# A PEER decoder layer: 192 instead of 128 tokens by gathered expert rows, 320 in the dense part with v as stationary operand

## Chip, cores and metric

The kernel runs on one core of one Trainium2 chip. The metric is the device time of one execution in microseconds (us), the median of the runs shown; lower is better.

## What is computed

One decoder layer on 512 tokens of width 1024, in fp32: normed input projection, three groups of attention heads, output projection and residual, and then the PEER feed-forward, which is all that the change touches. Each token picks 16 of 16384 experts for each of 8 heads; an expert is one row of `u` and one of `v`.

```python
def peer_ffn(h, w_q, sub1, sub2, u, v):
    qry = (h @ w_q).reshape(B, S, PEER_HEADS, PEER_DKEY)
    ...
    v1, i1 = lax.top_k(s1, PEER_TOPK)
    v2, i2 = lax.top_k(s2, PEER_TOPK)
    ...
    top_s, pos = lax.top_k(cand, PEER_TOPK)
    expert = jnp.take_along_axis(cand_idx, pos, axis=-1)
    gate = jax.nn.softmax(top_s, axis=-1)
    ...
        a = jnp.einsum('cd,ced->ce', x_c, u[e_c])
        w = jax.nn.gelu(a.astype(jnp.float32), approximate=False).astype(x_c.dtype) * g_c
        return jnp.einsum('ce,ced->cd', w, v[e_c])
```

## The kernel before

The 512 tokens are four chunks of 128. Projection, attention and output projection come first (to about 300 us) and are untouched. After them the kernel treats the feed-forward in two ways.

**Chunk 0 by gathered rows.** `route` (L411) finds 128 experts and gates for every token. `gather_all` (L477) is a Python generator of 256 steps. A u step has GpSimd (POOL) issue an indirect DMA that brings, for slot s, one row of u for each of the 128 tokens into a tile `row` (512 KB, four buffers, L473); VectorE (DVE) multiplies it with the normed tokens `hg` and sums (L480). After 128 of them a Gelu and a product give the weights `gw`, and 128 v steps add weighted rows of v into `ga[0]` (L487).

**Chunks 1 to 3 densely.** All 16384 experts are computed for 384 tokens, in 128 blocks b of 128 experts. A *first product* (`a_block`, L515) multiplies a block of u with the tokens: 24 matmuls of 384 moving columns into a bank `t`, then a Gelu on ScalarE (ACT). All products have three matmuls per operand pair (`mm3`, L91), because an fp32 operand is split into a high and a low part: ScalarE copies the high part, VectorE subtracts (`split`, L83; `u_parts`, L508). The first products of blocks 0 to 63 are computed early and parked in HBM (`ad`). The gates come from one-hots: VectorE makes two one-hot rows per token (L584, L585), TensorE (PE) multiplies them (L588), and the resulting table goes to HBM (`gd`, L590). A *second product* (`w_block`, L616) loads a block of v and its slice of the gate table (`gt`), multiplies Gelu and gate into `w` (L632), splits v and w, and adds `w` times v into six PSUM banks that hold 384 x 1024 outputs: 18 matmuls of 512 columns, with w as stationary operand (L635 to L638). I call the stretch of second products the dense part.

The order on each engine comes from a scheduler that simulates the program; every engine then runs its instructions in that fixed order, and SP issues nearly all plain DMAs in order. The early first products each release one gather step (L596); the rest of the generator is emptied at the end of the program text (L654), and the scheduler mixes those steps with the dense part.

Of the kernel before, what the change touches and what calls it, by code (L numbers as in the profile page):

```python
# [22 lines left out]
P = 128  # L23
S = 512
# [22 lines left out]
GR = 1.0  # L47
TD = P * len(DC)
GROUPS = ((0, 1, 2), (3, 4, 5), (6, 7))
# [5 lines left out]
def layer_kernel(ctx, tc, x, xT, memT, mem, w_in, w_kv, w_out, w_q, cols, qk_gain, g_bc, subT, bias_tab,  # L55
# [9 lines left out]
    st = ctx.enter_context(tile_pool(name="st", bufs=8))  # L65
    xd = [dram.tile([P, D], F32, name=f"xd{c}") for c in range(NT)]
    gd = dram.tile([TD // GT, P, NK, GT], F32, name="gd")
# [51 lines left out]
    def quarters(t):  # L119
        return t.rearrange("p (a b) -> p a b", b=P)  # L120
# [232 lines left out]
    def mix_out(chunks, yT, rg, hT, name):  # L353
        n_c = len(chunks)
        with tile_pool(name=f"wo{name}", bufs=2) as wo:
# [26 lines left out]
            for i, c in enumerate(chunks):  # L382
                if i == 1:
                    for k2 in range(KD // 2):
                        w_piece(0, k2)
                DMA.dma_start(xd[c], xs[i])
# [83 lines left out]

    def gather(table, s_):
        row = gr.tile([P, D], F32, tag="row", name="row")
        G.indirect_dma_start(out=row, out_offset=None, in_=table,  # L473
                             in_offset=bass.IndirectOffsetOnAxis(ap=exp_g[:, s_:s_ + 1], axis=0))
        return row

    def gather_all():  # L477
        for s_ in range(NSLOT):
            row = gather(u, s_)
            V.scalar_tensor_tensor(row, row, 1.0, hg, ALU.mult, ALU.mult, accum_out=av[:, s_:s_ + 1])  # L480
            yield
        ge = peer.tile([P, NSLOT], F32, name="ge")
        A.activation(ge, av, AF.Gelu)
        V.tensor_mul(gw, ge, gate_g)
        for s_ in range(NSLOT):
            row = gather(v, s_)
            V.scalar_tensor_tensor(ga[0], row, gw[:, s_:s_ + 1], ga[0], ALU.mult, ALU.add)  # L487
            yield

# [24 lines left out]

    def a_block(b):  # L515
        us = halves.pop(b)
        ap = bank("t")[:, :TD]
        for k in range(KD):
            mm3(ap, [t[:, k, :] for t in us], [t[:, k, S - TD:] for t in hT], k == 0, k == KD - 1)
        ag = ub.tile([P, TD], F32, tag="ag", name="ag", bufs=3)  # L520
        A.activation(ag, ap, AF.Gelu)  # L521
        return ag

    with tile_pool(name="qa", bufs=1) as qa, tile_pool(name="qp", bufs=2) as qp:
        mix_out([GC] + DC, yT, rg, hT, "l")
        G.memset(ga[0], 0.0)
        rp = ctx.enter_context(tile_pool(name="rp", bufs=1, side="right"))
        sub = qa.tile([P, 2 * PH, NK], F32, name="sub", bufs=1)
        for n in range(4):
# [25 lines left out]
            for i in range(4):  # L555
                m = 4 * n + i
                acc = bank("s")[:, :TD]
                for k in range(KD):
                    mm3(acc, [t[:, i, k % 2, :] for t in w[k // 2]], [t[:, k, S - TD:] for t in hT],
                        k == 0, k == KD - 1)  # L560
                qy = qp.tile([P, TD], F32, tag="qy", name="qy")
                A.activation(qy, acc, AF.Copy)
                sc = quarters(bank("o"))[:, 0:len(DC), :]
                for j in range(len(DC)):
                    T.matmul(sc[:, j, :], qy[:, j * P:(j + 1) * P], sub[:, m, :], start=True, stop=True)
                sx = qa.tile([P, 4, P], F32, tag="sx", name="sx", bufs=SCB)[:, 0:len(DC), :]
# [34 lines left out]
    with tile_pool(name="vb", bufs=2) as vb:  # L601
        acc = [[bank("ssssoo"[2 * c + n]) for n in range(2)] for c in range(len(DC))]
        inl, spl = (list(range(r0, r1, NB)) for r0, r1 in ((NSP, NK), (0, NSP)))
# [12 lines left out]
        def w_block(n, b, ag):  # L616
# [17 lines left out]
            split(ws[0], ws[1], w)  # L634
            for ci_ in range(len(DC)):  # L635
                for k in range(2):
                    mm3(acc[ci_][k], [t[:, ci_ * P:(ci_ + 1) * P] for t in ws],
                        [t[:, k * 512:(k + 1) * 512] for t in vs], n == 0, n == NK - 1)  # L638

        pend = None  # L640
        for n, b in enumerate(order):
            if b >= NSP:
                for a in (b, later.get(b)):
                    if a is not None and a not in halves and a >= loaded:
                        u_parts(a, a % 2, V)
                        loaded = a + 1
                ag = a_block(b)
# [8 lines left out]
        for c in [GC] + DC:  # L656
            xr = vb.tile([P, D], F32, tag="xr", name="xr", bufs=3)
            DMA.dma_start(xr, xd[c])
            if c == GC:
                V.tensor_add(xr, xr, ga[0])  # L660
            else:
                for k in range(2):
                    sl = xr[:, k * 512:(k + 1) * 512]
                    V.tensor_add(sl, sl, acc[DC.index(c)][k])
            DMA.dma_start(out[c * P:(c + 1) * P, :], xr)

# [58 lines left out]
```

## Time and profile before

| | us |
|---|---|
| median of 3 runs (1699.19 to 1702.47) | 1700.5 |
| the profiled execution | 1706.93 |
| its span, first to last instruction | 1705.2 |
| busy TensorE / VectorE / ScalarE / GpSimd | 1615.1 / 1322.7 / 675.1 / 500.4 |
| DMA, 390.04 MB | mean 229 GB/s |

The span is that of the profiled execution. Busy time of TensorE is modelled, and successive matmuls overlap, so durations of single matmuls are not their cost; the distance between two starts is. `PEclk` is the clock that TensorE was granted, as a share of 2.4 GHz. "out<-in" names the tiles an instruction writes and reads; a matmul's are output, moving and stationary operand.

### The profile page before, as it was taken

What the parts mean: (1) busy time and instruction counts of PE and PEld (TensorE: products, weight loads), DVE (VectorE), ACT (ScalarE), POOL (GpSimd) and SP (SyncE); (2) the same over time, 40 slices, a digit from 0 to 9 for tenths busy, and PEclk for the clock granted to TensorE, in tenths of its full rate; (3) what the DMA queues carried; (4) which work ended last, traced back from release to release, by engine and by line L of the source; (5) the groups of instructions that cost most, each with busy time, mean ns of one, the idle gap of its engine ahead of it and who ended that gap; (6) DMA issues with size and microseconds to landing.
All of it is one profiled execution on the core that took longest, in us unless ns stands there. A gap on an engine that the chain in (4) does not pass through costs nothing.

```text
span 1705.2 us, 23275 instructions
## 1 busy us (share of the span) xinstructions
PE 1615.1 (95%) x8045; PEld 1402.8 (82%) x8045; DVE 1322.7 (78%) x3271; ACT 675.1 (40%) x1031; POOL 500.4 (29%) x338
## 2 busy tenths in 40 slices
PE   7999989998999898988786999999999999999998
PEld 6886667998999897887565888888888888888887
DVE  6656746699999999989996788788887878844444
ACT  7345534233434435444452333333333333333332
POOL 4320013252325232654103343334443333200000
PEclk9999989999999999998897999999999999999999
DMA  8302034133888675675439999999998999854542
GB/s 320 117 27 106 1 115 157 50 112 104 273 282 283 229 279 199 222 278 197 197 141 386 328 349 326 318 345 332 346 333 326 329 349 336 302 195 150 184 146 79
DMA packets 164373, 390.04 MB, mean 229 GB/s; under 512 B 12704, under 2 KB 87456, under 8 KB 161568
## 3 DMA queue, kind: packets, MB, share of 16 engines
q1 hardware_dynamic: 127392, 254.33, 42.9%
q0 software_dynamic: 36864, 134.23, 22.0%
q8 instruction: 63, 1.03, 0.2%
q14 instruction: 54, 0.44, 0.1%
HBM read 346.57 MB, written 41.94 MB: 228 GB/s over the span
## 4 chain that ended last, share of the span: by engine, by line
PE 68%; DVE 25%; DMA 4%; ACT 2%; issue 2%; POOL 0%; SPq 0%; DVEq 0%; ACTq 0%
PE s L93 9%; PE s L95 9%; PE s L94 9%; PE t L93 7%; PE t L95 7%; PE t L94 7%; PE o L94 4%; PE o L93 4%; PE o L95 4%; DVE row L480 4%; DVE o L585 4%; DVE yT L85 3%; PE s L588 3%; DVE o L584 3%; PE o L328 2%
## 5 line engine op out<-in xcount | busy, mean ns | idle before, releaser
L93 PE MATMUL t<-hT,yT 128*128 128x384 f32 x1024 | 350.0, 342 | 25.1 <-ACT ag L521 25.0
L95 PE MATMUL t<-hT,yT 128*128 128x384 f32 x1024 | 349.3, 342 | 11.8 <-DVE yT L85 11.8
L94 PE MATMUL t<-hT,yT 128*128 128x384 f32 x1024 | 348.5, 340 | 0.0
L473 POOL DMA_INDIRECT row<-u,exp_g x128 | 189.8, 1483 | 409.4 <-DVE row L480 292.1
L84 ACT ACTIVATE yT<-flat 128x1024 fp32r<-128x1024 f32 x128 | 135.7, 1060 | 264.3 <-PE t L94 130.6
L473 POOL DMA_INDIRECT row<-v,exp_g x128 | 165.3, 1292 | 255.4 <-DVE ga L487 235.7
L93 PEld LDWEIGHTS t<-hT,yT 128*128 128x128 f32 x1024 | 194.7, 190 | 31.6 <-ACT ag L521 27.1
L85 DVE TENSOR_TENSOR yT<-vr,yT 128x1024 fp32r<-128x1024 f32 x128 | 156.4, 1222 | 69.0 <-ACT yT L84 65.7
L95 PEld LDWEIGHTS t<-hT,yT 128*128 128x128 f32 x1024 | 194.6, 190 | 17.4 <-DVE yT L85 14.1
L85 DVE TENSOR_TENSOR yT<-flat,yT 128x1024 fp32r<-128x1024 f32 x128 | 164.7, 1288 | 52.4 <-ACT yT L84 44.6
L94 PE MATMUL s<-yT,ws 128*128 128x512 f32 x512 | 202.7, 396 | 0.0
L94 PEld LDWEIGHTS t<-hT,yT 128*128 128x128 f32 x1024 | 194.7, 190 | 4.5
L84 ACT ACTIVATE ws<-w 128x384 fp32r<-128x384 f32 x128 | 67.1, 525 | 330.2 <-issue 127.3
L95 PE MATMUL s<-yT,ws 128*128 128x512 f32 x512 | 195.2, 396 | 0.0
L480 DVE SCALAR_TENSOR_TENSOR row<-row,hg 128x1024 f32<-128x1024 f32 x128 | 163.7, 1288 | 13.9 <-DMA row<-u,exp_g 13.7
L84 ACT ACTIVATE yT<-vr 128x1024 fp32r<-128x1024 f32 x128 | 134.5, 1051 | 95.9 <-PE o L95 68.2
L93 PE MATMUL s<-yT,ws 128*128 128x512 f32 x512 | 167.8, 396 | 0.0
L588 PE MATMUL s<-o,o 128*128 128x128 f32 x768 | 154.7, 315 | 11.3 <-DVE o L585 8.4
L487 DVE SCALAR_TENSOR_TENSOR ga<-row,gw,ga 128x1024 f32<-128x1024 f32 x128 | 163.6, 1278 | 1.7 <-DMA row<-v,exp_g 1.0
L588 PEld LDWEIGHTS s<-o,o 128*128 128x128 f32 x768 | 122.1, 199 | 42.6 <-issue 18.8
L85 DVE TENSOR_TENSOR ws<-w,ws 128x384 fp32r<-128x384 f32 x128 | 70.5, 556 | 95.1 <-ACT ws L84 90.9
L585 DVE TENSOR_SCALAR o<-iota,iT 128x128 f32<-128x128 f32 x384 | 131.7, 343 | 0.0
(264 smaller groups left out, 2861.0 us busy)
## 6 DMA issues: line engine op xcount, KB each, us to landing
flat<-uT SPq DMA_DIRECT2D x128, 512.0 KB
vr<-v SPq DMA_DIRECT2D x128, 512.0 KB
gd<-stage SPq DMA_DIRECT2D x12, 2048.0 KB
gt<-gd SPq DMA_DIRECT2D x32, 768.0 KB
ad<-ag SPq DMA_DIRECT2D x64, 192.0 KB
agr<-ad SPq DMA_DIRECT2D x64, 192.0 KB
wraw<-w_in SPq DMA_DIRECT2D x8, 1024.0 KB
flat<-w_q SPq DMA_DIRECT2D x16, 512.0 KB
```

The lines of the kernel that those rows point to most:

```text
L84: A.activation(hi, src, AF.Copy)
L85: return (e_lo or V).tensor_sub(lo, src, hi.bitcast(F32))
L93: T.matmul(o, ah, bh, start=start, stop=False)
L94: T.matmul(o, ah, bl, start=False, stop=False)
L95: T.matmul(o, al, bh, start=False, stop=stop)
L328: T.matmul(o_ps[:, q0:W], l, r, start=n_ == 0, stop=n_ == len(mms) - 1)
L473: G.indirect_dma_start(out=row, out_offset=None, in_=table, in_offset=bass.IndirectOffsetOnAxis(ap=exp_g[:, s_:s_ + 1], axis=0))
L480: V.scalar_tensor_tensor(row, row, 1.0, hg, ALU.mult, ALU.mult, accum_out=av[:, s_:s_ + 1])
L487: V.scalar_tensor_tensor(ga[0], row, gw[:, s_:s_ + 1], ga[0], ALU.mult, ALU.add)
L584: V.tensor_scalar(o1[:, j, :], iota, i1, None, ALU.is_equal)
L585: V.tensor_scalar(o2[:, j, :], iota, i2, gate, ALU.is_equal, ALU.mult)
L588: T.matmul(gp[:, j, :], o1[:, j, :], o2[:, j, :], start=True, stop=True)
```

## The change

64 tokens more go by gathered rows: the first half (`HX`) of chunk 1. Their 128 slots are folded so that all 128 partitions work: partitions 0 to 63 hold slots 0 to 63 of a token, partitions 64 to 127 its slots 64 to 127. So `gather_all` has 64 more u steps and 64 more v steps, which accumulate in `ga[1]`, and its order is u of chunk 0, u of the half, v of chunk 0, v of the half. The normed half tokens go through HBM (`hd`) into both halves of `hx`; the experts and gates get there by one ScalarE copy and one DMA each in `route`. At the end the two halves of `ga[1]` are brought together by a DMA into `other`.

The dense part has `TD` = 320 tokens. First products have 320 moving columns and use one fixed bank, `only`. Second products turn the operands around: v is stationary, `w` with 320 columns moves, and the result is transposed, 8 chunks of 128 output columns by 320 tokens. Seven chunks have a bank each; the eighth is in two pieces, 192 and 128 columns, in what is left of two of these banks. At the end the result is copied to `yo`, transposed in 128x128 squares and added to x. All residual loads stand behind the last gather in the program's end.

```diff
-TD = P * len(DC)
+HX = P // 2
+DX = DC[0]
+T0 = (DX * P) + HX
+TQ = P * len(DC)
+TD = S - T0
...
+                if c == DX:
+                    DMA.dma_start(hd, h[0:HX, :])
...
+        if c == DX:
+            for to, src in zip(extra, (ei, gt)):
+                A.activation(to[0:HX, :], src[0:HX, 0:HX], AF.Copy)
+                DMA.dma_start(to[HX:P, :], src[0:HX, HX:P])
...
+    def gather_all(hx, avx, gwx, exp_x, gate_x):
+        sets = ((NSLOT, exp_g, hg, av, gate_g, gw, ga[0]), (HX, exp_x, hx, avx, gate_x, gwx, ga[1]))
...
+        for n, ex, h, a_, gate, g_, to in sets:
+            for s_ in range(n):
+                row = gather(u, ex, s_)
+                V.scalar_tensor_tensor(row, row, 1.0, h, ALU.mult, ALU.mult, accum_out=a_[:, s_:s_ + 1])
+                yield
+            ge = peer.tile([P, n], F32, name=f"ge{n}")
+            A.activation(ge, a_, AF.Gelu)
+            V.tensor_mul(g_, ge, gate)
+        for n, ex, h, a_, gate, g_, to in sets:
+            for s_ in range(n):
+                row = gather(v, ex, s_)
+                V.scalar_tensor_tensor(to, row, g_[:, s_:s_ + 1], to, ALU.mult, ALU.add)
+                yield
...
-    def a_block(b):
+    def a_block(b, to=None):
         us = halves.pop(b)
-        ap = bank("t")[:, :TD]
+        ap = (bank("t") if to is None else to)[:, :TD]
...
+        for i in range(2):
+            DMA.dma_start(hx[i * HX:(i + 1) * HX, :], hd)
...
-            for q in range(P // GT):
+            for q in range(HX // GT if c == DX else 0, P // GT):
...
-        acc = [[bank("ssssoo"[2 * c + n]) for n in range(2)] for c in range(len(DC))]
+        acc = [bank(tag) for tag in "ssssoot"]
+        only = bank("t")
+        parts = [[(acc[j][:, 0:TD], 0, TD)] for j in range(KD - 1)]
+        parts.append([(acc[0][:, TD:S], 0, S - TD), (acc[1][:, TD:2 * TD - (S - TD)], S - TD, TD)])
...
-            for ci_ in range(len(DC)):
-                for k in range(2):
-                    mm3(acc[ci_][k], [t[:, ci_ * P:(ci_ + 1) * P] for t in ws],
-                        [t[:, k * 512:(k + 1) * 512] for t in vs], n == 0, n == NK - 1)
+            for j in range(KD):
+                for o, t0, t1 in parts[j]:
+                    mm3(o, [t[:, j * P:(j + 1) * P] for t in vs], [t[:, t0:t1] for t in ws],
+                        n == 0 and j < KD - 1, n == NK - 1 and j > 1)
...
+        for j in range(KD):
+            V.memset(yo[j][:, TD:], 0.0)
+            for o, t0, t1 in parts[j]:
+                if j % 2:
+                    A.activation(yo[j][:, t0:t1], o, AF.Copy)
+                else:
+                    V.tensor_copy(yo[j][:, t0:t1], o)
+
+        def emit(r0, rows, terms):
             xr = vb.tile([P, D], F32, tag="xr", name="xr", bufs=3)
...
+        other = vb.tile([P, D], F32, tag="xr", name="other", bufs=3)
+        DMA.dma_start(other[0:HX], ga[1][HX:P, :])
+        emit(GC * P, P, [(every, ga[0])])
+        emit(DX * P, HX, [(every, ga[1]), (every, other)])
...
+                for j in range(4):
+                    T.transpose(ps[:, j * P:(j + 1) * P], yo[4 * k + j][:, i:i + P], ident)
```

The scheduler gives the program a new order. On VectorE, before the change, the last gather multiply of all (L487, into `ga`) stands in the middle of the dense part, ahead of the addition of the residual (L660); the `w` of 32 further second products is still to come.

```order
L632 TENSOR_TENSOR w<-agr,gt 128x384
L487 SCALAR_TENSOR_TENSOR ga_1416<-row,gw,ga_1416 128x1024
L85 TENSOR_TENSOR ws_12954<-w,ws_12953 128x384
L85 TENSOR_TENSOR yT_1442<-vr,yT_1441 128x1024
L660 TENSOR_TENSOR xr<-xr,ga_1416 128x1024
L85 TENSOR_TENSOR yT_1442<-flat,yT_1441 128x1024
L632 TENSOR_TENSOR w<-ag,gt 128x384
```

After the change, the end of VectorE's order reads so (`ws` is the last second product's split, L502 a gather multiply, L687 a copy of a finished bank, L693 the additions at the end):

```order
L90 TENSOR_TENSOR yT_1440<-vr,yT_1439 128x1024
L90 TENSOR_TENSOR ws_15252<-w,ws_15251 128x320
L502 SCALAR_TENSOR_TENSOR ga_1414<-row,gw,ga_1414 128x1024 x2
L687 COPY yo_16250<-s 128x320
L687 COPY yo_16252<-o 128x320
L502 SCALAR_TENSOR_TENSOR ga_1414<-row,gw,ga_1414 128x1024
L687 COPY yo_16254<-t 128x320
L687 COPY yo_16248<-s 128x320
L502 SCALAR_TENSOR_TENSOR ga_1414<-row,gw,ga_1414 128x1024 x27
L502 SCALAR_TENSOR_TENSOR ga_1415<-row,gwx,ga_1415 128x1024 x64
L693 TENSOR_TENSOR xr<-xr,ga_1414 128x1024
L693 TENSOR_TENSOR xr<-xr,ga_1415 64x1024
```

94 gather multiplies stand behind the last split of the dense part, where none stood.

On SP the program ended, before, with the loads of the last blocks and three stores of finished tokens:

```order
L627 DMA vr<-v 128x1024 x7
L619 DMA agr<-ad_131 128x384
L627 DMA vr<-v 128x1024
L665 DMA out<-xr 128x1024 x3
```

and now ends so, where `other` reads the finished `ga[1]`:

```order
L651 DMA vr<-v 128x1024
L698 DMA other<-ga_1415 64x1024
L691 DMA xr<-xd 128x1024
L691 DMA xr<-xd 64x1024
L694 DMA out<-xr 128x1024
L694 DMA out<-xr 64x1024
L691 DMA xr<-xd 128x1024 x2
L691 DMA xr<-xd 64x1024
L694 DMA out<-xr 128x1024 x2
L694 DMA out<-xr 64x1024
```

The loads of x moved from the middle of the dense part to behind the last gather. On TensorE the last second product, formerly rows of 512 columns such as `L95 MATMUL o<-yT_1441,ws_14420 128x512`, ends with the eighth chunk's short pieces:

```order
L99 MATMUL t<-ws_15252,yT_1439 128x320
L100 MATMUL t<-ws_15251,yT_1440 128x320
L98 MATMUL s<-ws_15251,yT_1439 128x192
L99 MATMUL s<-ws_15252,yT_1439 128x192
L100 MATMUL s<-ws_15251,yT_1440 128x192
L98 MATMUL s<-ws_15251,yT_1439 128x128
L99 MATMUL s<-ws_15252,yT_1439 128x128
L100 MATMUL s<-ws_15251,yT_1440 128x128
```

The moving operand is `ws` where it was `yT`, and one second product has 27 matmuls where it had 18.

## Rows read from the trace of the kernel before

**Rows 1.** Stretches: us; busy us (xcount) PE, PEld, DVE, ACT, POOL; PEclk; DMA share; GB/s.
```profile
390.00:730.00 340.00, 318.47 (x1847) 307.25 (x1846) 335.98 (x1112) 143.55 (x183) 120.92 (x67) 0.98 0.69 233
730.00:892.00 162.00, 140.00 (x706) 114.34 (x704) 154.80 (x526) 74.65 (x78) 44.88 (x24) 0.92 0.54 204
892.00:910.00 18.00, 0.00 (x0) 0.00 (x0) 9.74 (x18) 1.37 (x2) 11.14 (x8) 0.57 0.89 327
910.00:1057.00 147.00, 146.36 (x686) 127.45 (x687) 114.14 (x169) 53.35 (x74) 50.66 (x43) 0.98 0.96 345
1057.00:1480.00 423.00, 423.00 (x2007) 366.91 (x2006) 342.50 (x372) 148.12 (x202) 165.50 (x129) 1.00 0.94 334
1480.00:1700.00 220.00, 219.57 (x1031) 188.84 (x1029) 103.82 (x128) 74.27 (x100) 0.00 (x0) 1.00 0.48 155
```

**Rows 2.** Line 487: ns min/median/max, first and last start us, shapes.
```profile
L487 DVE SCALAR_TENSOR_TENSOR ga<-row,gw,ga x128: 1272/1277/1287, 1073.9 to 1486.6; 128x1024 f32<-128x1024 f32 x128
```

**Rows 3.** Timeline, TensorE, two products' first rows; columns start us, us, engine, line.
```profile
1560.47 0.33 PE L93 MATMUL t<-hT,yT 128*128 128x384 f32 x1
...
1564.66 0.39 PE L93 MATMUL s<-yT,ws 128*128 128x512 f32 x1
...
1568.87 0.33 PE L93 MATMUL t<-hT,yT 128*128 128x384 f32 x1
```

**Rows 4.** Timeline, VectorE, one-hot stage, 36 pairs between these.
```profile
797.79 0.27 DVE L584 TENSOR_SCALAR o<-iota,iT 128x128 f32<-128x128 f32 x1
...
814.11 0.27 DVE L584 TENSOR_SCALAR o<-iota,iT 128x128 f32<-128x128 f32 x1
```

**Rows 5.** Timeline, VectorE, gather multiplies before the dense part, splits inside.
```profile
902.66 1.23 DVE L480 SCALAR_TENSOR_TENSOR row<-row,hg 128x1024 f32<-128x1024 f32 x1 [6.67 <-DMA row<-u,exp_g]
903.81 0.08 DVE L480 DVE_READ_ACCUMULATOR row<-row,hg 128x1 f32 x1
...
907.95 1.22 DVE L480 SCALAR_TENSOR_TENSOR row<-row,hg 128x1024 f32<-128x1024 f32 x1 [1.41 <-DMA row<-u,exp_g]
...
1057.21 1.21 DVE L85 TENSOR_TENSOR yT<-vr,yT 128x1024 fp32r<-128x1024 f32 x1
1058.35 0.54 DVE L632 TENSOR_TENSOR w<-agr,gt 128x384 f32<-128x384 f32 x1
```

**Rows 6.** Timeline, SP and ACT at the start, the first load.
```profile
1.64 0.42 SPq L150 DMA_DIRECT2D xtr<-xT  x1
...
4.51 1.28 ACT L88 ACT_TABLE_LOAD   x1 [4.51 <-DMA xtr<-xT]
```

**Rows 7.** TensorE's first and last matmul of the dense part; stores.
```profile
910.64 0.69 PE L93 MATMUL t<-hT,yT 128*128 128x384 f32 x1 [18.69 <-ACT ag L521]
...
1699.17 0.40 PE L95 MATMUL o<-yT,ws 128*128 128x512 f32 x1
...
L665 SPq DMA_DIRECT2D out<-xr x4: 332/340/344, 1491.9 to 1701.0; - x4
```

**Rows 8.** Timeline, TensorE, attention, five fp32 transposes.
```profile
142.90 0.71 PE L315 MATMUL t<-ident,p 128*128 128x128 f32 x5
143.45 0.81 PE L296 MATMUL s<-kT,qT 128*128 128x384 f32 x2
```

**Rows 9.** Groups: xcount, busy us, mean ns, idle us before and releaser.
```profile
L473 POOL DMA_INDIRECT row<-v,exp_g x128 | 165.3, 1292 | 255.4 <-DVE ga L487 235.7 <-issue 8.2 <-DVE row L480 8.0
...
L521 ACT ACTIVATE ag<-t 128x384 f32<-128x384 f32 x128 | 61.0, 478 | 31.0 <-PE t L95 16.9 <-issue 11.8 <-ACT stage L589 0.8
```

**Rows 10.** The page's queue of GpSimd: packets, MB, share.
```profile
q0 software_dynamic: 36864, 134.23, 22.0%
```

**Rows 11.** Timeline, GpSimd, gathers of u before the dense part.
```profile
897.10 0.94 POOL L473 DMA_INDIRECT row<-u,exp_g  x1 [0.30 <-issue]
...
899.58 0.94 POOL L473 DMA_INDIRECT row<-u,exp_g  x1 [0.31 <-issue]
904.16 1.81 POOL L473 DMA_INDIRECT row<-u,exp_g  x1 [3.64 <-DVE row L480]
```

More of the change, by code (lines that the diff above doesn't have):

```diff
@@ L65, in layer_kernel @@
     st = ctx.enter_context(tile_pool(name="st", bufs=8))
-    xd = [dram.tile([P, D], F32, name=f"xd{c}") for c in range(NT)]
+    hd = dram.tile([HX, D], F32, name="hd")
+    xd = dram.tile([S, D], F32, name="xd")
     gd = dram.tile([TD // GT, P, NK, GT], F32, name="gd")
@@ L385, in mix_out @@
                         w_piece(0, k2)
-                DMA.dma_start(xd[c], xs[i])
+                DMA.dma_start(xd[c * P:(c + 1) * P, :], xs[i])
                 r = row_rstd(xs[i], f"rh{c}")
@@ L409, in top16, with route @@
             V.max_index(idx[q][:, 8:16], vals[q][:, 8:16], rest[q])
-    def route(c, dst=None, q0=0, nq=PH):
+    def route(c, dst=None, q0=0, nq=PH, extra=()):
         qs = slice(q0, q0 + nq)
@@ L469, in route, with gather @@
         A.activation(dst, tp, AF.Copy)
[L471 to L488, printed above, removed]
+    def gather_all(hx, avx, gwx, exp_x, gate_x):
+        sets = ((NSLOT, exp_g, hg, av, gate_g, gw, ga[0]), (HX, exp_x, hx, avx, gate_x, gwx, ga[1]))
+        def gather(table, ex, s_):
+            row = gr.tile([P, D], F32, tag="row", name="row")
+            G.indirect_dma_start(out=row, out_offset=None, in_=table,
+                                 in_offset=bass.IndirectOffsetOnAxis(ap=ex[:, s_:s_ + 1], axis=0))
+            return row
+        for n, ex, h, a_, gate, g_, to in sets:
[11 more added lines that the diff above has]
+                yield
     lp = ctx.enter_context(tile_pool(name="lp", bufs=1, side="right"))
@@ L525, in layer_kernel @@
         mix_out([GC] + DC, yT, rg, hT, "l")
-        G.memset(ga[0], 0.0)
+        for t in ga:
+            G.memset(t, 0.0)
         rp = ctx.enter_context(tile_pool(name="rp", bufs=1, side="right"))
+        hx = rp.tile([P, D], F32, name="hx")
+        avx, gate_x, gwx = (rp.tile([P, HX], F32, name=n_) for n_ in ("avx", "gate_x", "gwx"))
+        exp_x = rp.tile([P, HX], I32, name="exp_x")
+        for i in range(2):
+            DMA.dma_start(hx[i * HX:(i + 1) * HX, :], hd)
         sub = qa.tile([P, 2 * PH, NK], F32, name="sub", bufs=1)
@@ L556, in layer_kernel @@
                 m = 4 * n + i
-                acc = bank("s")[:, :TD]
+                acc = bank("s")[:, :TQ]
                 for k in range(KD):
-                    mm3(acc, [t[:, i, k % 2, :] for t in w[k // 2]], [t[:, k, S - TD:] for t in hT],
+                    mm3(acc, [t[:, i, k % 2, :] for t in w[k // 2]], [t[:, k, S - TQ:] for t in hT],
                         k == 0, k == KD - 1)
-                qy = qp.tile([P, TD], F32, tag="qy", name="qy")
+                qy = qp.tile([P, TQ], F32, tag="qy", name="qy")
                 A.activation(qy, acc, AF.Copy)
@@ L589, in layer_kernel @@
                     A.activation(stage[:, :, t4:t4 + 4].rearrange("p e t -> p t e"), gp, AF.Copy)
-                DMA.dma_start(gd[ci_ * (P // GT) + q], stage)
+                DMA.dma_start(gd[(c * P - T0) // GT + q], stage)
         for b in range(NSP):
@@ L646, in layer_kernel @@
                         loaded = a + 1
-                ag = a_block(b)
+                ag = a_block(b, only)
             else:
@@ L655, in layer_kernel @@
             pass
-        for c in [GC] + DC:
-            xr = vb.tile([P, D], F32, tag="xr", name="xr", bufs=3)
[L658 to L665, printed above, removed]
+        yo = [vb.tile([P, TQ], F32, tag=f"yo{j}", name=f"yo{j}", bufs=1) for j in range(KD)]
+        for j in range(KD):
[6 more added lines that the diff above has]
+        def emit(r0, rows, terms):
+            xr = vb.tile([P, D], F32, tag="xr", name="xr", bufs=3)
+            DMA.dma_start(xr[0:rows], xd[r0:r0 + rows, :])
+            for sl, t in terms:
+                V.tensor_add(xr[0:rows, sl], xr[0:rows, sl], t[0:rows])
+            DMA.dma_start(out[r0:r0 + rows, :], xr[0:rows])
+        every = slice(0, D)
+        other = vb.tile([P, D], F32, tag="xr", name="other", bufs=3)
+        DMA.dma_start(other[0:HX], ga[1][HX:P, :])
+        emit(GC * P, P, [(every, ga[0])])
+        emit(DX * P, HX, [(every, ga[1]), (every, other)])
+        for i in range(0, TD, P):
+            terms = []
+            for k in range(2):
+                ps = bank("so"[k])
+                for j in range(4):
+                    T.transpose(ps[:, j * P:(j + 1) * P], yo[4 * k + j][:, i:i + P], ident)
+                terms.append((slice(k * 512, (k + 1) * 512), ps))
+            emit(T0 + i, min(P, TD - i), terms)
 def _bias_table():
```

6 lines of the change are left out of this document (3 added, 3 removed).

## Prediction, made blind

> **What bounds the kernel now.** I read the page's queue table for sizes, the table of stretches first, then the matrix engine's timeline in the dense part, then the gather rows of GpSimd and VectorE, then the last microseconds. In the table of stretches [rows 1] VectorE is full from 390 to 892 us (336 of 340, 155 of 162): it splits u, multiplies gathered rows and builds the one-hots. From 892 to 910 TensorE stands still while the last gate tables go out and come back. From 910 to 1480 TensorE is busy to the last microsecond, and DMA moves 334 to 345 GB/s at a share of 0.94 to 0.96. After 1480 GpSimd has nothing left and DMA falls to 155 GB/s: the gathers are over, their last multiply starts at 1486.6 [rows 2], and TensorE alone sets the end. So today the gathers are wholly beside the dense part. The dense part is a row of matmuls at full clock (1.00): one first product takes 4.19 us, one second product 4.21 [rows 3].
>
> **The change, part by part.**
>
> *Ahead of the dense part.* 64 tokens fewer get one-hots. Between the two one-hot rows stand 36 pairs in 16.32 us, 0.453 us a pair [rows 4]; 64 pairs are 29.0 us of a full VectorE. In VectorE's order 92 u multiplies stand ahead of the first weight product where 82 stood, and 70 u splits where 71 stood. An operation of either kind takes 1.14 to 1.15 us from start to start [rows 5]: nine more cost 10.3. Net -19 us (bounds -29 and 0, if waits eat it). The copies and small transfers of `extra`, `hd` and `hx` are once per launch; SP's u loads stand behind two of them, with seven issued ahead at the stage's start, and I cost them at nothing; uncovered they are two loads of 2.9 us [rows 6].
>
> *The dense part on TensorE.* By the order 58 first products are left after the first weight product; now 59. Before: 58 x 4.19 + 128 x 4.21 = 782 us, against 789 from 910.6 to the last matmul's end at 1699.6 [rows 7]. The 7 us over I keep. Per column a matmul takes 4.19/24/384 = 0.455 ns or 4.21/18/512 = 0.457 ns, so one of 320 columns takes 0.1455 us, and a first product 24 x 0.1455 = 3.49. A second product has 21 of 320 columns and, for the eighth output chunk split over two banks, three of 192 and three of 128. How long a short one with its own weight load takes, this data type does not show. Lower bound: per column 0.087 and 0.058, 0.44 us for the six. Upper bound: the 384-column matmuls start 0.175 us apart with a load each, 1.05 us for six. I take the nearest row, fp32 128x128 transposes through the array, with a load each: five starts in 0.55 us, 0.11 each [rows 8], 0.66 for six. A second product is then 21 x 0.1455 + 0.66 = 3.71 (3.50 to 4.11). The part is 59 x 3.49 + 128 x 3.71 + 7 = 688 us (661 to 739): -101.
>
> One PSUM bank instead of two now takes the first products. The Gelu that empties it is 0.48 us [rows 9], and in the order second products mostly stand between two first ones: 3.7 us of cover, so nothing; with no cover it would be about 59 x 0.5 = 30 us. VectorE stays below the bound: per second product one 1.14 v split, about 0.8 for the two 320-wide operations, 0.46 u splits and 1.56 gather rows of 1.2, some 4.3 us, against 688/128 = 5.4. DMA: per second product 1.56 rows and 1.46 tables of 0.524 MB (134.23 MB over 256 rows [rows 10]) and 0.25 of gates and products, 1.83 MB, 340 GB/s, as now.
>
> *The gathers.* 384 rows instead of 256, and here the order decides: VectorE runs its instructions in program order, and that has at most two gather multiplies between dense operations. When the last second product's operands are split, 94 v multiplies remain, and the next operations (`yo` copies) wait for the last matmul. 92 stand behind them, with nothing beside them. What one costs alone no row shows. Below: GpSimd started three in 2.48 us, 1.24 apart [rows 11], and the multiply takes 1.28 [rows 2]; 1.28. Above: with four buffers, the row issued at 899.58 was used at 907.95, with its use and restart 9.9 us, 2.5 per row, amid table traffic [rows 5, 11]. I take GpSimd's mean 1.29 plus its 0.30 between issues [rows 9, 11], 1.6. Four rows are there already. 92 x 1.6 - 4 x 0.3 = **+146 us** (117 to 230), where the gathers cost the end nothing before.
>
> The Trainium skill (DMA: Bandwidth & Descriptors, Anatomy of one DMA) fits 2.0 us plus bytes over 436 GB/s per transfer, 3.2 us for one row. By an estimate from that page the round of four buffers is 1.29 + 3.2 + 1.28 + 0.3 = 6.1 us, 1.52 per row, and the sum 7 us smaller. No run here shows a row alone.
>
> *The end.* Before: the last matmul ends at 1699.6 and the span at 1705.2, 5.6 us, of which the last store, issued at 1701.0, has 4.2 [rows 7]. Now SP's `other` waits for the last gather, and all five loads of x stand behind it on SP; the dense tokens' loads then wait for buffers. By the first load of the kernel (1.64 to 4.51 [rows 6]) a load is 2.9 us: 0.8 us behind it the second xr lands (3.7), three adds of 1.2 (7.3), a buffer comes free, load (10.2), the next loads wait for the stores' ends (about 9 and 11.6, so 14.5), two adds 1.4, store 4.2: 20 us. +14 (bounds +6 and +20). The transposes (24 matmuls) lie beside the gathers.
>
> Sum: -19 - 101 + 146 + 14 = **+40 us** on the profiled execution of 1706.9 (span 1705.2 and 1.7 around it). The median of the runs is 1700.5, 6.4 below, so I forecast 1740. Changes under about 0.2%, 3.4 us, can't be told from none.
>
> **The rivals.**
> A. *Matmuls at their column rate.* At 384 columns a matmul takes 0.0146 us over its columns at 2.4 GHz, at 512 0.0206; this excess shrinks with the width, and with v stationary it may go. The 320-column ones would take 0.133: 59 x 3.2 + 128 x 3.46 + 7 = 639 us, 49 less, 1691: faster. It decides from a dense part below some 645 us. Against it: a load per matmul stays, and both shapes show the excess.
> B. *Tail at the buffers' best pace*, 1.28 us a row: 29 us less, 1711. For it: nothing else moves on the queues. Against: a round of four needs issue, transfer and use one behind the other.
> C. *GpSimd slowed by VectorE.* An issue with VectorE at work beside it took 1.81 us, those in its 6.67 us pause 0.94 [rows 5, 11]. If each tail row took 1.81 + 0.30, it is 92 x 0.51 = 47 us more, 1787. The Trainium skill (SBUF — State Buffer, Who interferes with whom) has a VectorE instruction with two SBUF inputs shut out a GpSimd instruction that reads SBUF; these rows agree, but the mean over all 128, most of them beside a busy VectorE, is 1.29 [rows 9].
> D. *Short matmuls at 0.175 us*: 128 x 0.39 = 50 us more, 1790; against it the 0.11 of [rows 8].
>
> **How the numbers follow.** Forecast 0.54, A 0.10, B 0.12, C 0.15, D 0.05, other causes 0.04. The forecast's own spread is about 20 us either side (epilogue, head, pace). The range 1700 to 1785 leaves out A, D and the far part of C. Faster: A and a sliver of B, 0.11; same: 0.06 from the edges of B and the forecast; slower 0.83.
>
> **What would show it.** The profile after should have TensorE done near 1580 us, then some 140 us in which only GpSimd issues `row<-v` and VectorE adds to `ga`, about 1.6 us a row; 320-column matmuls 0.145 apart; short ones 0.11; the span's last 20 us SP loads and stores. Wrong would be: gathers that end with TensorE, a row under 1.3 us, or a dense part below 645.

## The result, and the profile after

| | before | after |
|---|---|---|
| median of the runs (lowest to highest) | 1701.2 (1699.19 to 1702.47) | 1781.5 (1778.93 to 1783.45) |
| the profiled execution | 1706.93 | 1778.93 |
| its span | 1705.2 | 1777.2 |

The changed kernel takes 1.047 times as long (95% interval 1.045 to 1.049): slower, as forecast, and inside the range, but by 80 us in the medians where 40 were forecast. Between the two profiled executions it is 72.0 us; the other 8 are that before's profiled execution lay 5.7 above its median and after's 2.6 below. All that follows explains the 72.

First the table of stretches, with the columns of [rows 1]: the wait ahead of the dense part, the dense part, the tail, the end.

```profile
868.00:886.00 18.00, 0.00 (x0) 0.00 (x0) 10.27 (x26) 1.27 (x3) 10.32 (x8) 0.60 0.93 342
886.00:1578.00 692.00, 691.55 (x4877) 691.55 (x4878) 560.34 (x742) 264.33 (x377) 241.26 (x199) 1.00 0.94 335
1584.00:1754.00 170.00, 0.00 (x0) 0.00 (x0) 114.55 (x90) 0.00 (x0) 105.41 (x87) 0.51 0.81 272
1755.00:1777.00 22.00, 1.12 (x4) 0.72 (x4) 7.33 (x9) 0.00 (x0) 0.00 (x0) 0.50 0.64 203
```

The dense part is what it was in [rows 1], only shorter: TensorE without a gap, DMA at 0.94 and 335 GB/s. Then TensorE has nothing left, its clock falls to half, and for 170 us VectorE and GpSimd work alone, neither of them full (115 and 105 us of 170), and DMA is not full either (0.81, 272 GB/s). In [rows 1] TensorE was busy through the last 220 us and GpSimd had nothing to do.

TensorE's timeline: the first matmul of the dense part, then the rows of one second product, and the last matmul, one of the eighth chunk's short pieces. They answer to [rows 3] and [rows 7].

```profile
886.45 0.63 PE L98 MATMUL t<-hT,yT 128*128 128x320 f32 x1 [18.67 <-ACT ag L536]
...
1562.80 0.31 PE L98 MATMUL t<-ws,yT 128*128 128x320 f32 x1
1562.95 0.31 PE L99 MATMUL s<-ws,yT 128*128 128x320 f32 x1
...
1565.01 0.25 PE L98 MATMUL s<-ws,yT 128*128 128x192 f32 x1
...
1565.32 0.24 PE L98 MATMUL s<-ws,yT 128*128 128x128 f32 x1
...
1565.62 0.81 PE L98 MATMUL s<-ws,yT 128*128 128x320 f32 x4
...
1566.56 0.31 PE L98 MATMUL t<-ws,yT 128*128 128x320 f32 x1
...
1580.55 0.28 PE L100 MATMUL s<-ws,yT 128*128 128x128 f32 x1
```

Fifteen 320-column matmuls start between 1562.80 and 1565.01, 0.147 us each; the six short ones take 0.61 together, the other six 320-column ones 0.94; one product is 1566.56 - 1562.80 = 3.76 us. The dense part runs from 886.45 to 1580.8, 694.4 us, and takes no wait at its start that before did not have (18.67 us idle, 18.69 in [rows 7]).

The timeline of GpSimd and VectorE in the tail, where each buffer's round can be followed:

```profile
1689.82 1.32 POOL L487 DMA_INDIRECT row<-v,exp_x  x1 [0.31 <-issue]
1691.44 0.94 POOL L487 DMA_INDIRECT row<-v,exp_x  x1 [0.30 <-issue]
...
1693.21 0.94 POOL L487 DMA_INDIRECT row<-v,exp_x  x1 [0.82 <-DVE ga L502]
...
1695.55 0.94 POOL L487 DMA_INDIRECT row<-v,exp_x  x1 [1.41 <-DVE ga L502]
1696.22 1.28 DVE L502 SCALAR_TENSOR_TENSOR ga<-row,gwx,ga 128x1024 f32<-128x1024 f32 x1 [0.94 <-DMA row<-v,exp_x]
1697.67 2.60 DVE L502 SCALAR_TENSOR_TENSOR ga<-row,gwx,ga 128x1024 f32<-128x1024 f32 x2 [0.16 <-DMA row<-v,exp_x]
1697.78 1.99 POOL L487 DMA_INDIRECT row<-v,exp_x  x1 [1.29 <-DMA row<-v,exp_x]
```

The row issued at 1689.82 is used at 1696.22, and its buffer is filled again from 1697.78: a round of 7.96 us here, for one of four buffers. The table of waits over 1585 to 1753 (what waited for what; us, times, longest) shows a ring:

```profile
DVE ga L502 <- DMA row<-v,exp_x: 39.5, 45, 1.7
POOL row L487 <- DVE ga L502: 38.8, 39, 2.0
```

VectorE waits for rows, and GpSimd waits for VectorE to empty a buffer. So I take the loop, and no single engine, to be the bound; the experiments test that.

The end, on SP and VectorE: the last add, and what the epilogue does with it.

```profile
1753.52 1.28 DVE L502 SCALAR_TENSOR_TENSOR ga<-row,gwx,ga 128x1024 f32<-128x1024 f32 x1 [1.13 <-DMA row<-v,exp_x]
1754.88 0.47 SPq L698 DMA_DIRECT2D other<-ga  x1
1755.40 1.27 SPq L691 DMA_DIRECT2D xr<-xd  x2
1759.70 2.35 DVE L693 TENSOR_TENSOR xr<-xr,ga 128x1024 f32<-128x1024 f32 x2 [4.90 <-DMA xr<-xd]
...
1763.94 2.99 SPq L691 DMA_DIRECT2D xr<-xd  x3
1768.65 0.69 DVE L693 TENSOR_TENSOR xr<-xr,s 128x512 f32<-128x512 f32 x1 [5.35 <-DMA xr<-xd]
...
1769.97 3.88 SPq L694 DMA_DIRECT2D out<-xr  x3
```

Two loads in a row, each with some 5 us of VectorE idle behind it, then the stores: 1754.8 to 1777.2 is 22.4 us.

The four stretches give the whole difference. The ends are those rows, of before from [rows 7]:

| term | forecast | measured | from |
|---|---|---|---|
| ahead of the dense part | -19 | -24.2 | 910.64 to 886.45 |
| dense part | -101 | -94.6 | 789.0 to 694.4 |
| tail of gathers | +146 | +174.0 | 1580.8 to 1754.8, 92 rows |
| end | +14 | +16.8 | 5.6 to 22.4 |
| sum | +40 | +72.0 | spans 1705.2 to 1777.2 |

The tail holds 28 of the 32 us that were missed: 1.89 us a row instead of 1.6.

### The profile page after: what moved, and what is told of

Same layout as the page of the kernel before. It is cut to its first block, busy times and chain, and to the rows that moved or that the text cites. A ratio compares the mean times of both kernels' runs of the same rounds, so it can differ in the third digit from the quotient of the medians.

```text
span 1777.2 us, 25653 instructions
## 1 busy us (share of the span) xinstructions
PE 1466.7 (83%) x9093; PEld 1356.0 (76%) x9093; DVE 1430.8 (81%) x3350; ACT 645.3 (36%) x1023; POOL 618.0 (35%) x467
## 3 DMA queue, kind: packets, MB, share of 16 engines
q8 instruction: 71, 1.16, 0.2%
## 4 chain that ended last, share of the span: by engine, by line
PE 62%; DVE 22%; DMA 8%; issue 4%; POOL 2%; ACT 2%; SPq 0%; DVEq 0%; POOLq 0%; ACTq 0%
PE s L99 8%; PE s L100 8%; PE s L98 8%; PE t L98 7%; PE t L100 7%; PE t L99 7%; DMA row<-v,exp_x 4%; DVE row L494 4%; DVE yT L90 3%; PE s L609 3%; PE o L98 3%; PE o L99 3%; PE o L100 3%; DVE o L606 3%; DVE o L605 2%
## 5 line engine op out<-in xcount | busy, mean ns | idle before, releaser
L98 PE MATMUL t<-hT,yT 128*128 128x320 f32 x1024 | 327.0, 319 | 34.7 <-ACT ag L536 30.9
L100 PE MATMUL t<-hT,yT 128*128 128x320 f32 x1024 | 324.4, 318 | 12.9 <-DVE yT L90 12.9
L99 PE MATMUL t<-hT,yT 128*128 128x320 f32 x1024 | 322.9, 315 | 0.0
L487 POOL DMA_INDIRECT row<-u,exp_g x128 | 164.2, 1283 | 387.7 <-DVE row L494 279.3
L487 POOL DMA_INDIRECT row<-v,exp_g x128 | 157.1, 1227 | 241.5 <-DVE ga L502 223.8
L98 PEld LDWEIGHTS t<-hT,yT 128*128 128x128 f32 x1024 | 198.0, 193 | 37.5 <-ACT ag L536 33.4
L99 PE MATMUL s<-ws,yT 128*128 128x320 f32 (+2 forms) x768 | 220.7, 297 | 0.0
L100 PE MATMUL s<-ws,yT 128*128 128x320 f32 (+2 forms) x768 | 210.3, 297 | 0.0
L100 PEld LDWEIGHTS t<-hT,yT 128*128 128x128 f32 x1024 | 197.4, 193 | 15.6 <-DVE yT L90 15.6
L99 PEld LDWEIGHTS t<-hT,yT 128*128 128x128 f32 x1024 | 197.7, 193 | 0.0
L98 PE MATMUL s<-ws,yT 128*128 128x320 f32 (+2 forms) x768 | 184.8, 293 | 0.0
L502 DVE SCALAR_TENSOR_TENSOR ga<-row,gw,ga 128x1024 f32<-128x1024 f32 x128 | 163.9, 1281 | 15.2 <-DMA row<-v,exp_g 14.8
L99 PEld LDWEIGHTS s<-ws,yT 128*128 128x128 f32 x768 | 144.0, 189 | 0.0
L100 PEld LDWEIGHTS s<-ws,yT 128*128 128x128 f32 x768 | 141.5, 189 | 0.0
L609 PE MATMUL s<-o,o 128*128 128x128 f32 x640 | 130.1, 315 | 6.0 <-DVE o L606 2.8
```

The costliest lines, as they stand in the source:

```text
L98: T.matmul(o, ah, bh, start=start, stop=False)
L99: T.matmul(o, ah, bl, start=False, stop=False)
L100: T.matmul(o, al, bh, start=False, stop=stop)
L487: G.indirect_dma_start(out=row, out_offset=None, in_=table, in_offset=bass.IndirectOffsetOnAxis(ap=ex[:, s_:s_ + 1], axis=0))
L502: V.scalar_tensor_tensor(to, row, g_[:, s_:s_ + 1], to, ALU.mult, ALU.add)
L609: T.matmul(gp[:, j, :], o1[:, j, :], o2[:, j, :], start=True, stop=True)
```

## The experiments

Ten kernels. The first three ask whether the buffers' round sets the tail and what the tail is worth; the next two separate the round from VectorE's part in it and look for the next limit; three try the cure, alone and with more; the last two measure a row alone. "Per row" is the time from the last dense matmul's end to the last add's end over the adds between, as 174.0/92 = 1.89 above.

### Seven row buffers in the tail

The `flat` buffers are free once the last u block is split; in the tail they take three rows of seven.

```diff
-            row = gr.tile([P, D], F32, tag="row", name="row")
+            k = turns[0]
+            turns[0] += 1
+            if k >= 288 and 4 <= k % 7 < 7:
+                row = fp.tile([P, D], F32, tag="flat", name="rowf")
+            else:
+                row = gr.tile([P, D], F32, tag="row", name="row")
```

> The kernel after the change, with seven row buffers instead of four in the last 96 gather steps (three more come from the freed tiles of the u loads); the order of the dense part stays. Theory (a row costs the round of four buffers, 7.6 us in the profile after, over four = 1.9): with seven buffers the round is no longer the limit, GpSimd's own pace is (mean issue 1.21 + 0.30), so a row costs about 1.5 us and the stretch of 170 us shrinks to about 140; ratio to before about 1.027. Rival (GpSimd's issues are slowed by VectorE's adds, whatever the buffers): a row stays at 1.9, ratio 1.047. Rival (the DMA queue cannot carry gathers alone faster than its 272 GB/s): stays at 1.9 too, with GpSimd waiting less for VectorE.

Measured: 1739.0 us, 1.021 times before (1.018 to 1.024). The tail in the table of stretches:

```profile
1584.00:1715.00 131.00, 2.45 (x20) 2.15 (x20) 120.17 (x97) 0.80 (x3) 98.26 (x89) 0.52 0.97 359
```

94 adds in 132.4 us, 1.41 per row. With nothing edited but the number of buffers, the DMA engines carry 359 GB/s instead of 272 and VectorE is busy 120 of 131 us. So neither the queue nor the engines were at their limit with four buffers. 92 x (1.89 - 1.41) is 44 us, and the time fell by 42.5.

### Three row buffers everywhere

```diff
-    gr = ctx.enter_context(tile_pool(name="gr", bufs=4, side="right"))
+    gr = ctx.enter_context(tile_pool(name="gr", bufs=3, side="right"))
```

> The kernel after the change with three row buffers instead of four everywhere. The order has 79 u steps ahead of the dense part instead of 92 and leaves 108 v steps behind the last split. Theory (round over buffers): a row costs 7.6 / 3 = 2.5 us in the tail, 106 x 2.5 = 265 us instead of 175, the head 15 us shorter: about 1855 us, ratio 1.09. Rivals (GpSimd slowed by VectorE, or the queue's rate): 1.9 a row, 201 us, about 1795, ratio 1.055.

Measured: 1851.0 us, 1.087 times before (1.084 to 1.090), where the theory of the round has 1.09.

```profile
1600.00:1825.00 225.00, 0.00 (x0) 0.00 (x0) 127.40 (x100) 0.00 (x0) 97.89 (x98) 0.50 0.75 231
```

A hundred adds in 225 us, 2.25 per row, a round of 6.8 us of three buffers. Fewer buffers, a slower tail, at a DMA share of 0.75. That the total came out so close is partly luck: the tail is 239.6 us where the theory had 265, because the round among three is shorter than the 7.6 us among four, and the dense part starts 6 us later (892.6 against 886.4) where the theory had the head 15 us shorter.

### The half chunk's gathers left out

```diff
-        for n, ex, h, a_, gate, g_, to in sets:
+        for n, ex, h, a_, gate, g_, to in sets[:1]:
```

This stands in both loops, so 64 u and 64 v steps are gone: the 64 tokens of the half get no expert output.

> The kernel after the change without the 64 u steps and 64 v steps of the half chunk: those 64 tokens get no expert output; the dense part keeps its 320 tokens and v as stationary operand. The order has all 128 v steps done when 112 of 128 second products have begun. Theory (the dense part is worth its 94 us, the loss is the uncovered gathers alone): dense part 690 us, no tail, end about 20 us after the last matmul: about 1600 us, ratio 0.94. Rival (the dense part is no shorter without the extra gathers, or the turned operands cost elsewhere): above 1640.

Measured: 1600.4 us, 0.941 times before (0.938 to 0.943). The page's row of GpSimd's queue:

```profile
q0 software_dynamic: 36864, 134.23, 23.2%
```

and the dense part in the table of stretches:

```profile
884.00:1586.00 702.00, 694.50 (x4888) 694.13 (x4889) 529.38 (x654) 264.98 (x377) 213.31 (x164) 0.99 0.88 310
```

The queue moves what it moved in [rows 10], and TensorE is busy for the 694 us that it has in the changed kernel. So the 320-token dense part with the head is worth 6% by itself, and the 64 tokens' gathers cost 1781.5 - 1600.4 = 181 us, all of it behind the last matmul: the tail's 174 us and an end of 22.4 instead of 9.6 us, less 6 us by which the dense part ends later without them (1587.1 against 1580.8).

### The tail's adds taken from VectorE

```diff
-                V.scalar_tensor_tensor(to, row, g_[:, s_:s_ + 1], to, ALU.mult, ALU.add)
+                if n == NSLOT and s_ < 98:
+                    V.scalar_tensor_tensor(to, row, g_[:, s_:s_ + 1], to, ALU.mult, ALU.add)
+                else:
+                    A.activation(row, row, AF.Copy, scale=g_[:, s_:s_ + 1])
```

The last 94 rows of v are scaled by ScalarE and not added: those sums are missing from the output.

> The kernel after the change in which the last 94 gathered v rows are only scaled by ScalarE (copy with scale) and not added by VectorE, so VectorE is idle in the tail and those 94 weighted rows are missing from the result. Four buffers as before. Theory (round of four: issue 1.21, 1.48 to the first packet, 2.33 of transfer, 0.65 until the use, 1.29 of use, 0.67 until the buffer's next issue, 7.6 in all): only the use gets shorter, 1.29 to 1.05, so a row costs about 1.85 instead of 1.9 and the time falls by about 6 us, ratio 1.043. Rival (VectorE's adds slow GpSimd's issues): the mean issue falls from 1.21 to 0.94 and with it the waits between issues, a row costs 1.65 or less and the time falls by 23 us or more, ratio 1.033 or below.

Measured: 1769.2 us, 1.040 times before (1.036 to 1.044). The group of GpSimd's issues in the tail of the changed kernel (1585 to 1753), and then in the tail of this one (1600 to 1750):

```profile
L487 POOL DMA_INDIRECT row<-v,exp_x x64 | 78.5, 1226 | 45.4 <-DVE ga L502 28.6 <-issue 10.4 <-DMA row<-v,exp_x 6.5
```

```profile
L487 POOL DMA_INDIRECT row<-v,exp_x x59 | 55.3, 937 | 48.5 <-ACT row L505 44.6 <-issue 3.9
L505 ACT ACTIVATE row<-row,gwx 128x1024 f32<-128x1024 f32 x56 | 64.2, 1147 | 33.6 <-DMA row<-v,exp_x 32.2
```

Without VectorE at work GpSimd's issue is 0.94 us instead of 1.23, and the use is 1.15 instead of 1.28. From 1600 to 1750 one use follows another after 1.76 us on average, where it was 1.91 in the changed kernel: between the theory's 1.85 and the rival's 1.65, and worth 14 us over 92 rows. So VectorE's adds do lengthen the issues, and a row feels part of that.

The 12 us by which the time fell do not measure this, and that they lie near 14 is luck. Nothing is added to `ga` in this tail, so the loads of x, the last additions and the stores no longer wait for it: the span ends 2.3 us behind the last use instead of 22.4. Against that, the dense part ended at 1591.9 instead of 1580.8, and 97 rows stood behind it instead of 92.

### Ten row buffers in the tail

```diff
...
+            if k >= 288 and 4 <= k % 10 < 7:
+                row = fp.tile([P, D], F32, tag="flat", name="rowf")
+            elif k >= 288 and k % 10 >= 7:
+                row = late[0].tile([P, D], F32, tag="vr", name="rowv", bufs=3)
```

> As the run with seven buffers in the tail, with ten (three more from the v loads' tiles). Theory: with seven the buffers no longer bound the row but GpSimd's issue pace, 1.11 + 0.30, and the queue (0.524 MB at 360 GB/s, 1.45): ten change little, ratio to before 1.018 to 1.021. Rival (the buffers still bind at seven): a row falls from 1.48 to the adds' 1.28, some 18 us less, ratio 1.010.

Measured: 1736.2 us, 1.021 times before (1.017 to 1.025): within the noise of seven. A row costs 1.33 us (95 adds in 126.1 us) instead of 1.41.

```profile
1584.00:1710.00 126.00, 2.71 (x23) 2.24 (x22) 121.61 (x97) 0.94 (x3) 86.80 (x85) 0.53 0.94 364
```

VectorE is busy 121.6 of 126 us and DMA carries 364 GB/s. From seven buffers on other limits hold: 1.28 us of VectorE for each row, and a DMA share of 0.94 to 0.97.

### Seven row buffers from the dense part on

```diff
-            row = gr.tile([P, D], F32, tag="row", name="row")
...
+            if k >= 70 and k % 7 >= 4:
+                row = late[0].tile([P, D], F32, tag="rowx", name="rowx", bufs=3)
+            else:
+                row = gr.tile([P, D], F32, tag="row", name="row")
...
-            xr = vb.tile([P, D], F32, tag="xr", name="xr", bufs=3)
+            xr = vb.tile([P, D], F32, tag="vr", name="xr", bufs=3)
```

In VectorE's order 173 of the 192 v adds then stand ahead of the last split of `w`, where 98 stood (the expectation's 169 and 96 are four and two short).

> The kernel after the change with seven row buffers from the dense part on (three more in the pool of the dense part; the loads of x at the end use the buffers of the v loads). The scheduler then mixes in more gathers: 169 of 192 v steps stand ahead of the last split instead of 96, 23 behind it. Theory 1 (the dense part was bound by TensorE and DMA has room above 335 GB/s): dense part 690 to 720 us with 270 MB instead of 232 (380 GB/s), tail 23 rows x 1.5 = 35: about 1640 us, ratio 0.965. Theory 2 (DMA at a share of 0.94 is full at 345 GB/s): dense part 780 us, tail 35: about 1722, ratio 1.012.

Measured: 1692.1 us, 0.994 times before (0.991 to 0.996): 5% under the changed kernel, and 0.6% under the kernel before, little more than level with it. It fell between the two theories. Two stretches of its dense part:

```profile
1100.00:1400.00 300.00, 287.42 (x2017) 285.18 (x2015) 258.64 (x314) 107.71 (x154) 132.42 (x103) 1.00 0.98 359
1400.00:1620.00 220.00, 202.01 (x1410) 199.72 (x1410) 200.66 (x217) 75.32 (x108) 119.11 (x89) 1.00 1.00 370
```

TensorE's first dense matmul on its timeline:

```profile
901.56 0.63 PE L98 MATMUL t<-hT,yT 128*128 128x320 f32 x1 [26.48 <-ACT ag L543]
```

and, from the table of waits, what held TensorE longest after that (900 to 1646):

```profile
PE s L98 <- ACT yT L89: 31.6, 21, 1.6
```

More gathers beside the dense part, but now its DMA share is 0.98 to 1.00 and TensorE has gaps (202 us of 220), most of them behind `yT`, ScalarE's first copy of a loaded block. The dense part takes 745 us, from 901.56 to 1647.0; the tail shrinks to 22 us. Against the changed kernel: head +15, dense part +51, tail -152, end +0.2, sum -86, and the spans differ by 85.8. The tail's work is not free beside the dense part: some 66 of the 152 us come back, in a head and a dense part that wait more. That the full DMA is the reason is argued from its share, not tested by itself.

### The kernel before with seven row buffers

The same edit in the kernel before (from its step 64 on).

> The kernel before the change with seven row buffers in the dense part. There the gathers were beside a full TensorE and ended 200 us ahead of it, so the row buffers bound nothing: within 0.5% of the kernel before (ratio 0.995 to 1.005). Rival (earlier gathers crowd the loads of u and v at a DMA share of 0.94): up to 1.01.

Measured: 1730.9 us, 1.017 times before (1.013 to 1.021). The theory was wrong, and the rival's "up to 1.01" too low. TensorE's first dense matmul:

```profile
917.97 0.69 PE L93 MATMUL t<-hT,yT 128*128 128x384 f32 x1 [28.02 <-ACT ag L528]
```

and a stretch of its dense part:

```profile
1200.00:1480.00 280.00, 268.17 (x1251) 227.80 (x1250) 221.90 (x236) 93.48 (x127) 102.11 (x79) 1.00 0.89 322
```

The dense part starts 7.3 us later, after a wait of 28.0 instead of 18.7 us, and takes 805.7 us instead of 788.9; between 1200 and 1480 alone TensorE is idle for 11.8 us, where [rows 1] had no gap. So extra row buffers by themselves cost this program something: the gathers crowd the loads, or the new order puts loads late; which of the two was not tried. The gain of the version above is therefore not in buffers as such. It is that the changed kernel had 92 uncovered rows to give them.

### Seven buffers, and GpSimd doing part of the early splits

On top of that version, GpSimd takes every fourth low part of u ahead of the dense part, to relieve VectorE.

```diff
-                u_parts(loaded, loaded % 4, V)
+                u_parts(loaded, loaded % 4, G if loaded % 4 == 1 else V)
```

> The kernel with seven buffers in the dense part, in which GpSimd computes every fourth low part of u ahead of the dense part (16 of 64) instead of VectorE, which is full there. The order has 78 u steps ahead of the dense part instead of 92 and 175 v steps ahead of its last split. Theory (the head is bound by VectorE, the dense part by DMA at 365 GB/s): the head is 30 x 1.14 = 34 us shorter, the dense part carries 14 rows more, 20 us: ratio 0.986. Rival (GpSimd's 2.4 us subtractions hold the gathers back, or share the path of VectorE's second input): no gain, ratio 0.994 or more.

Measured: 1712.3 us, 1.005 times before (1.002 to 1.008): a miss for the theory, inside the rival's bound, and 20 us slower than without the edit. TensorE's first dense matmul:

```profile
891.41 0.64 PE L98 MATMUL t<-hT,yT 128*128 128x320 f32 x1 [29.21 <-ACT ag L543]
```

a stretch of its dense part:

```profile
1200.00:1500.00 300.00, 273.82 (x1837) 269.82 (x1838) 259.14 (x285) 99.89 (x143) 146.69 (x111) 0.96 0.96 357
```

and the group of VectorE's gather multiplies ahead of it, 390 to 891, and behind it the same group of the version above, 390 to 901:

```profile
L501 DVE SCALAR_TENSOR_TENSOR row<-row,hg 128x1024 f32<-128x1024 f32 x78 | 111.2, 1444 | 14.3 <-DMA row<-u,exp_g 14.2
```

```profile
L501 DVE SCALAR_TENSOR_TENSOR row<-row,hg 128x1024 f32<-128x1024 f32 x92 | 120.5, 1316 | 13.7 <-DMA row<-u,exp_g 13.5
```

The head got 10 us shorter, but only 78 gather multiplies fit into it instead of 92, and each took 1.44 instead of 1.32 us. The rest moved into a dense part that DMA already filled, and that grew from 745 to 786 us. The theory had 20 us for those 14 rows. Of the 41 us, 21 are more idle time of TensorE (63 instead of 43 us) and 20 more busy time: over the whole dense part its granted clock is 0.97, where the version above had 1.00 without such drops. From 1350 to 1370, for one, TensorE was busy for 14.4 of 20 us, and from 1370.1 to 1380.3 it was granted 0.50, the lower level of 1.2 GHz.

### A row alone, and two

The last 48 rows all use one buffer; in the second kernel, two in turn (`338` and `kept[k % 2]`).

```diff
...
+            if k < 337:
+                row = gr.tile([P, D], F32, tag="row", name="row")
+                if k >= 336:
+                    kept.append(row)
+            else:
+                row = kept[k % 1]
```

> The last 48 rows all go through one row buffer, one after the other, so the distance between two adds is the round of a row alone. Theory (the forecast's 1.6 us a row was too small because up to four rows in flight slow one another down, not because a single row takes longer than it allowed): alone, the transfer takes about half of the 2.3 us it has from first to last packet among four, and the issue 0.94: a round near 6.2 us, against 7.6 for four in flight; the time is 1781 + 47 x (6.2 - 1.9) = about 1985. Rival (a fixed round, whatever is in flight): 7.6 us, 1781 + 47 x 5.7 = about 2050. By an estimate from the Trainium skill (DMA: Bandwidth & Descriptors, Anatomy of one DMA) the round would be 0.94 + 3.2 + 1.29 + 0.67 = 6.1 us.

> The last 48 rows go through two row buffers in turn. Theory (rows in flight slow one another): a round between that of one buffer and that of four, about 6.5 us, 3.25 a row, 1781 + 46 x 1.35 = about 1843. Rival (fixed round of 7.6): 3.8 a row, 1781 + 46 x 1.9 = about 1868.

Measured, one run each: 1964.7 and 1832.9 us. The timeline of GpSimd and VectorE with one buffer:

```profile
1850.48 1.28 DVE L511 SCALAR_TENSOR_TENSOR ga<-row,gwx,ga 128x1024 f32<-128x1024 f32 x1 [4.64 <-DMA row<-v,exp_x]
1852.04 0.94 POOL L496 DMA_INDIRECT row<-v,exp_x  x1 [4.99 <-DVE ga L511]
1856.53 1.28 DVE L511 SCALAR_TENSOR_TENSOR ga<-row,gwx,ga 128x1024 f32<-128x1024 f32 x1 [4.76 <-DMA row<-v,exp_x]
```

and with two:

```profile
1750.75 1.29 DVE L511 SCALAR_TENSOR_TENSOR ga<-row,gwx,ga 128x1024 f32<-128x1024 f32 x1 [1.46 <-DMA row<-v,exp_x]
...
1754.03 1.28 DVE L511 SCALAR_TENSOR_TENSOR ga<-row,gwx,ga 128x1024 f32<-128x1024 f32 x1 [1.99 <-DMA row<-v,exp_x]
...
1756.59 1.28 DVE L511 SCALAR_TENSOR_TENSOR ga<-row,gwx,ga 128x1024 f32<-128x1024 f32 x1 [1.28 <-DMA row<-v,exp_x]
```

With one buffer, use follows use after 6.05 us here; the mean of 40 is 5.9. With two, a buffer's uses at 1750.75 and 1756.59 are 5.84 apart. The rival of a fixed round of 7.6 falls; two rows do not yet lengthen each other's round, three and four do. The parts of the round, as means in the tails of five kernels, from the issues, the packets of GpSimd's queue and the adds in the traces:

| buffers | issue | to its first packet | first to last packet | to the use | use | to the next issue | round | per row |
|---|---|---|---|---|---|---|---|---|
| 1 | 0.94 | 0.71 | 2.26 | 0.43 | 1.28 | 0.27 | 5.9 | 5.9 |
| 2 | 0.94 | 0.71 | 2.32 | 0.43 | 1.28 | 0.27 | 5.9 | 3.0 |
| 3 | 1.00 | 1.03 | 2.83 | 0.33 | 1.29 | 0.35 | 6.8 | 2.3 |
| 4 | 1.21 | 1.47 | 2.33 | 0.66 | 1.29 | 0.68 | 7.6 | 1.9 |
| 7 | 1.11 | 2.37 | 1.85 | 1.16 | 1.28 | 2.21 | 10.0 | 1.4 |

My reason in the expectation was wrong in one point: the transfer itself is no quicker alone (2.26 us against 2.33 among four, and 2.83 among three and 1.85 among seven show no order). What grows from one buffer to four is the wait before the first packet (+0.76), the wait of a freed buffer for GpSimd (+0.41), the issue (+0.27) and the wait of a landed row for VectorE (+0.23).

## Why the prediction was right or wrong

**The kind of result was right.** The program's fixed order left 92 rows behind the last matmul, nothing covered them, and this tail outweighs what TensorE saved. Without the half's gathers the same program is 6% faster than before; with them it is 4.7% slower.

**The step that failed** is the price of a tail row: "I take GpSimd's mean 1.29 plus its 0.30 between issues, 1.6". Measured it is 1.89, which makes the tail 28 us longer. I took the pace at which GpSimd can issue when it always finds a free buffer. In the tail it waits for buffers, and the price is the round over four. Its lower bound (1.28) and upper bound (2.5) held it. The right kind of price was there, the round over four of [rows 5, 11], and I used it as the upper bound only; as a figure its 9.9 us, taken amid table traffic, is farther off than the 1.6, since the round in the tail is 7.6 us.

The estimate from the Trainium skill (DMA: Bandwidth & Descriptors, Anatomy of one DMA), a round of 6.1 us and 1.52 a row, is good for one row alone: the runs show 5.9, and 0.71 + 2.26 = 3.0 us from issue end to last packet, 3.4 to the use, where its fit gives 3.2. Divided by four it falls short, since with four rows under way the round is 7.6.

**The dense part** was forecast at 688 us and took 694.4. The 21 matmuls of 320 columns take 3.15 us, 0.150 each (forecast 0.1455), the six short ones 0.61 (0.66), a second product 3.76 (3.71); 128 x 0.05 is the 6 us. Costing the single bank for first products, the Gelu, and VectorE and DMA in this part at nothing was right: TensorE is busy 691.55 of 692 us.

**The head** gave 24 instead of 19 us, within the bounds of 0 and 29; but in the five kernels above that change only the tail the dense part starts between 885.2 and 892.6 us, so a few of these us are spread between executions. **The end** took 22.4 instead of 20: VectorE's two waits for loads are 4.9 and 5.35 us, and a load was priced at 2.9 from the first one of the kernel.

**The rivals.** A (matmuls at their column rate) needed a dense part below 645; it is 694.4. B (1.28 a row) fails with four buffers at 1.89; ten come near it (1.33). D needed 0.175 for a short matmul; it is 0.61/6 = 0.10. C comes to nearly the measured time, but by another way: it wanted 1.81 us for each issue, and the mean is 1.2. VectorE does lengthen the issues, from 0.94, and taking it away was worth some 14 us of the tail's 174, while three more buffers were worth 42 with VectorE busier than before. The rule behind C in the Trainium skill (SBUF — State Buffer, Who interferes with whom), that a VectorE instruction with two SBUF inputs shuts out a reading GpSimd, fits the 0.94 without VectorE's adds. It doesn't explain alone why the issues take about 1.0 with ten buffers, where VectorE is busier than with four.

## What to carry to other kernels

Work that rotates through a few buffers costs, where nothing covers it, the whole round (issue, transfer, use, reissue) over the number of buffers, not the pace of its busiest engine; and that round must be taken as it is with all buffers under way. So ask of each moved piece of work how much of it stands behind the last cover in the fixed order, and read its round from a stretch where the loop runs full and the queues carry what they will carry then. Covering it is worth something only as far as the covering stretch has room; here it had little, with a DMA share of 0.98 to 1.00.

## What the runs showed of the hardware

- One core's DMA held 359 to 370 GB/s over 220 to 300 us at a share of 0.98 to 1.00. The Trainium skill (DMA: Bandwidth & Descriptors, Where 436 GB/s comes from) gives about 358 as the HBM limit of a core, half of what two cores share; with one core at work these stretches are slightly above.
- A gathered row of 512 KB takes 2.3 us from first to last packet alone, with two and with four under way (2.8 with three); what grows from one to four is mainly the wait around it. Two buffers halve the time per row of one (5.9 to 3.0); four instead of three bring it only from 2.3 to 1.9.
- GpSimd's issue of a gather takes 0.94 us with VectorE idle beside it and 1.23 on average beside VectorE's adds in the tail with four buffers.
- More row buffers made the kernel before 1.7% slower.
